# Casts and scaling on GpSimd, twelve output products beside steps 10 to 15, and loads ordered behind transfers in a windowed attention

## The chip, the cores and the metric

The kernel runs on one core of one Trainium2 chip. A core has a matrix engine (TensorE, PE in the profile, with PEld for its weight loads), a vector engine (VectorE, DVE), an activation engine (ScalarE, ACT), a general engine (GpSimd, POOL) and an engine that here only starts transfers (SyncE, SP). Each engine works through its own list of instructions in order, and waits on semaphores for what other engines and transfers give it. They share an on-chip memory of 128 partitions (SBUF); TensorE writes its products to eight banks of accumulators (PSUM), which VectorE and ScalarE read. The metric is the device time of one launch in microseconds (us), and lower is better; each figure is a median of several runs.

## The reference

A trunk of two layers for one sequence of 512 tokens and 1024 features. Layer 0 mixes tokens by a gated unit; layer 1 by attention. Both then have a gated feed-forward part with a short convolution and a gated embedding. What matters here is layer 1's attention, cut to its core:

```python
q = (xn @ w_q).reshape(B, nb, BLOCK, N_KV_HEADS, GQA_GROUP, HEAD_DIM)
scores = einsum('bnikgd,bnjkd->bnkgij', q, kblk) * HEAD_DIM ** -0.5
scores = scores - slopes * dist           # a slope per head, distance in tokens
scores = where(valid, scores, -inf)       # window of 128, causal
m = maximum(max(scores), sink)            # a learned sink per head
e = exp(scores - m)
probs = e / (sum(e) + exp(sink - m))
out = einsum('bnkgij,bnjkd->bnikgd', probs, vblk)
return out.reshape(B, S, 1024) @ w_o
```

There are 16 query heads of 64 features in four groups; each group shares one head of keys and values. Tokens stand in four blocks of 128; a block sees itself and the block before it.

## The kernel before, in words

**Products of three.** Every float32 matrix is split into a high part (rounded to the type that TensorE multiplies fast, F32R) and a low part, the rest. A product of two is then three matmuls: high by high, high by low, low by high (`mm3`, line 175). Activations carry the letters h and l (`oh`, `ol` are the high and low half of attention's output, `o2` their list by 128 features: two to a head group). Weights come from HBM as float32.

**The planner of weights.** `pieces` lists all weight pieces in the order of use, 1 MB each as a rule; a piece has two units of 128x1024. `load` (line 122) starts a piece's transfer on SyncE's queue into a raw buffer (`wraw`). `pump` (line 133) makes the next units ready: `wh`, a cast on ScalarE (line 154), and `wl`, a subtraction on VectorE (line 155); it calls `load` for the piece that it needs. Four `wh` and four `wl` buffers go round. `chunk` hands a piece's units to the products. In attention's steps there is one raw buffer (`state["tags"] = [0]`), so that a load waits until both units of the piece before it have been subtracted.

**Attention's steps.** There are 16 steps, i = 4 g + n, for head group g and token block n. The loop from line 864 traces in each turn i: `scores(i)`; `fill(i)`, other products to lie beside the step; `mix(i - 2)`; `turn(i - 1)`; `weights(i)`. The loop ends two turns later, so 16 and 17 have no scores.

- `scores` (767): eight score products on TensorE (`sc`), a masked copy and four fused reductions with the slope on VectorE (784, 788; they write `prs`), four exponentials with their sums on ScalarE (793).
- `weights` (797): reciprocals of the sums, and the scaling of the four heads' 128x128 probabilities, the first on VectorE (807), three on ScalarE (805).
- `turn` (816): four transposes on TensorE (`tr`, 822), their split into `ph` and `pl` (ScalarE 252, VectorE 253), and for all but a sequence's first block two selections on GpSimd (830) for the block before.
- `mix` (835): two or four products with the values (`pv`, 844), a copy on ScalarE (848), two additions on VectorE (852), the high half `oh` on ScalarE (856) and the low half `ol` on GpSimd (857; the last step's on VectorE).

**What lies beside the steps.** The table `beside` (733) gives `fill` its work. Steps 0 to 9: `project`, the query products of groups 1 to 3 (`q`), 24 beside steps 0 and 1, and 12 beside each of 2 to 9. With a half group's last product `queries` (641) scales the result, splits it on ScalarE (657) and VectorE (658), and starts four transfers on SyncE's queue (661, 662), which lay the high and low halves out over the partitions; a group's scores need those of both halves. From step 10 on: `merge(m, k0, k1)` (720), the output products of 128 features m (`o`) over the inputs k0 to k1, three matmuls for each k. Inputs 2 g and 2 g + 1 are head group g's, so they need all four blocks' mixes of that group. A started `o` keeps its PSUM bank until its last product, behind the loop (line 884). `more` pumps one unit.

**Who sets the order.** A scheduler orders each engine's instructions at build time by priority, which is about the order of the program's text, and by when it expects operands and buffers to be free. `tc.high_priority()` moves scores, turn and weights ahead. So a step's scores can pass products that were traced before them, loads can pass transfers, and a product that is expected late is put behind others. On the chip the order is fixed.

Of the kernel before, what the change touches and what calls it, by code (L numbers as in the profile page):

```python
# [48 lines left out]
def tile_yoco(ctx: ExitStack, tc: tile.TileContext, t, out: bass.AP, out_b: bass.AP):  # L49
# [67 lines left out]

    units = [(i, q, lo, n) for i, p in enumerate(pieces) for q, (lo, n) in enumerate(p[2])]
    raws, ready = {}, {}
    state = {"raw": 0, "unit": 0, "next": 0, "tags": [0, 1, 2], "turn": 0, "pt": 0}  # L120

    def load(upto, queue=nc.sync):
        while state["raw"] < min(upto, len(pieces)):
            j = state["raw"]
            a, m = pieces[j][:2]
            tags = state["tags"]
            r = wp.tile([P, 2 * UNIT], F32, tag=f"r{tags[state['turn'] % len(tags)]}", bufs=1, name=f"wraw{j}")
            state["turn"] += 1
            queue.dma_start(r[:, :m].rearrange("p (c m) -> p c m", c=2) if j in paired else r[:, :m], a)
            raws[j] = r  # L130
            state["raw"] += 1

    def pump(upto):
        while state["unit"] < min(upto, len(units)):
            i, q, lo, n = units[state["unit"]]
            load(i + 1)
            u = state["unit"]
            own = pieces[i][3]
            if own:
                pool, *tags = own[q]  # L140
                wh, wl = (pool.tile([P, n], F32R, tag=tg, name=f"own{u}_{tg}") for tg in tags)
            else:
                wh = wp.tile([P, UNIT], F32R, tag="wh", bufs=WBUFS, name=f"wh{u}")
                wl = wp.tile([P, UNIT], F32R, tag="wl", bufs=WBUFS, name=f"wl{u}")
            if i in paired:
                whole = raws[i][:, : pieces[i][1]].rearrange("p (c k n) -> p k c n", c=2, n=256)
                src = whole[:, lo // S : (lo + n) // S]
                hi, low = (x[:, :n].rearrange("p (k c n) -> p k c n", c=2, n=256) for x in (wh, wl))
            else:
                src, hi, low = raws[i][:, lo : lo + n], wh[:, :n], wl[:, :n]  # L150
            if u == 0:
                nc.vector.tensor_copy(hi, src)
            else:
                nc.scalar.copy(hi, src)  # L154
            nc.vector.tensor_sub(low, src, hi.bitcast(F32))  # L155
            ready[u] = (wh, wl, n)
            state["unit"] += 1
# [17 lines left out]
    def mm3(ps, parts, xs, c0, n=P, first=True, last=True):  # L175

        for k, ((wh, wl, off), (xh, xl)) in enumerate(zip(parts, xs)):
            a, b = off + c0, off + c0 + n
            st = first and k == 0
            en = last and k == len(parts) - 1  # L180
            nc.tensor.matmul(ps, wh[:, a:b], xh, start=st, stop=False)  # L181
            nc.tensor.matmul(ps, wh[:, a:b], xl, start=False, stop=False)  # L182
            nc.tensor.matmul(ps, wl[:, a:b], xh, start=False, stop=en)  # L183

    def mm3t(ps, xs, parts, c0, n, tok, first=True, last=True):

# [454 lines left out]
    def queries(ps, g, j):  # L641
# [17 lines left out]
        for e, q in enumerate(res):  # L659
            me, it = sides[e], sides[1 - e]  # L660
            nc.sync.dma_start(q[me, :].bitcast(F32), hi[me, :])
            nc.sync.dma_start(q[it, :].bitcast(F32), qf[me, :])
        return res

    qs = {0: []}
# [63 lines left out]
    def more():  # L729
# [12 lines left out]
        7: [(project, 3, 0, 4, 8), (more,)],  # L742
        8: [(project, 3, 1, 0, 4)],
        9: [(project, 3, 1, 4, 8)],
        10: [(merge, 0, 0, 3), (more,)],
        11: [(merge, 0, 3, 4), (merge, 1, 0, 2), (more,)],
        12: [(merge, 1, 2, 4), (merge, 2, 0, 1)],
        13: [(merge, 2, 1, 4)],
        14: [(merge, 0, 4, 6), (merge, 1, 4, 6)],
        15: [(merge, 2, 4, 6)],  # L750
        16: [(merge, 3, 0, 6)],
        17: [(merge, 4, 0, 6)],
    }

    def fill(i):
        for f, *args in beside.get(i, []):
            f(*args)

    o2 = [[ap.tile([P, S], F32R, tag=f"a{x}{m}", name=f"o{x}{m}") for x in "hl"] for m in range(KD)]
    steps = [(g, n) for g in range(GROUPS) for n in range(NC)]  # L760
    live = {}
# [5 lines left out]
    def scores(i):  # L767
# [8 lines left out]
        for b in range(2):  # L776
            sc = psum(f"sc{i}_{b}").rearrange("p (e h k) -> p e h k", e=2, h=2)
            for j in range(2):
                o = sc[:, j].rearrange("p h k -> p (h k)")[:, :nk]
                q = qs[g][2 * b + j][:, n * P : (n + 1) * P]  # L780
                nc.tensor.matmul(o, q, kh[g // 2][:, g % 2, t0 : t0 + nk], start=True, stop=False)
                nc.tensor.matmul(o, q, kl[g // 2][:, g % 2, t0 : t0 + nk], start=False, stop=True)
# [14 lines left out]
    def weights(i):  # L797
# [4 lines left out]
        for e in range(GQ):  # L802
            a, r = pr[:, e, :P], ds[:, e : e + 1]
            if e:
                nc.scalar.activation(a, a, AF.Copy, scale=r)
            else:
                nc.vector.tensor_scalar_mul(a, a, r)
        live[i] = pr

    def pair(name):  # L810
# [45 lines left out]
            nc.scalar.copy(oh[:, cols], o[:, b, :])  # L856
            (nc.vector if i == last - 1 else nc.gpsimd).tensor_sub(ol[:, cols], o[:, b, :], oh[:, cols].bitcast(F32))

    last = len(steps)
    side = at.tile([P, 4 * S], F32, tag="vtl", name="side")  # L860
    fill(-1)
    state["tags"] = [0]
    pts4 = wp.tile([P, 4, S], F32R, tag="r1", bufs=1, name="pts4")
    for i in range(last + 2):
        if i < last:
            with tc.high_priority():
                scores(i)
# [242 lines left out]
```

## Time and profile before

| What | Value |
|---|---|
| median of 3 runs | 1141.03 us (1140.64 to 1141.64) |
| the profiled execution's own time | 1141.22 us |
| its span in the profile | 1139.5 us |
| granted TensorE clock | 0.998 |
| attention's steps, first scores to the last mix | about 591.8 to 686.3 us |

The profile is of one execution. Its page gives each engine's busy time; views of the trace give groups of instructions, stretches of time and single instructions with what ended the idle time before them ("0.80 <-DVE prs L807": 0.80 us idle, ended by VectorE's instruction of line 807 that writes `prs`). A matmul's duration overlaps that of the next, so the cost of one is the distance from start to start. Names come without buffer numbers: `wraw`, `wh`, `o`. L12 is line 12 of the kernel.

### The profile page before, as it was taken

How to read it: one execution, taken by the hardware profiler on the slowest of the kernel's cores; microseconds unless marked ns; L12 is line 12 of the kernel's file. 1: busy time of each engine (PE TensorE's matmuls, PEld its weight loads, DVE VectorE, ACT ScalarE, POOL GpSimd, SP SyncE). 2: the span in 40 equal slices, each digit the busy share in tenths (PEclk: the TensorE clock that was granted, in tenths of full speed). 3: DMA queues.
4: the chain of work that ended last, by engine and by line, in shares of the span. 5: the costliest groups of instructions: out<-in, count | busy, mean ns of one | idle time of the engine just before them, and what ended most of it. 6: DMA issues, size and time to landing. Idle time of an engine off the chain costs nothing.

```text
span 1139.5 us, 13604 instructions
## 1 busy us (share of the span) xinstructions
PE 1127.0 (99%) x5266; PEld 940.5 (83%) x5266; DVE 749.6 (66%) x1158; ACT 530.0 (47%) x875; POOL 107.7 (9%) x175
## 2 busy tenths in 40 slices
PE   9999999999999999999999999999999999999997
PEld 7888888888888888888898878888888888888896
DVE  7366477763677367557988977777636763675675
ACT  6533344441344234445657985444313432355562
POOL 2000200000000000021213343000000000000222
PEclk9999999999999999999999999999999999999999
DMA  8422323223223322432224315223223233224302
GB/s 298 145 83 74 111 75 111 101 85 111 78 98 102 111 76 86 134 107 79 74 75 129 93 38 185 98 88 111 78 107 110 66 102 111 93 80 160 111 1 75
DMA packets 25776, 115.41 MB, mean 101 GB/s; under 512 B 2920, under 2 KB 8176, under 8 KB 16240
## 3 DMA queue, kind: packets, MB, share of 16 engines
q1 hardware_dynamic: 25152, 113.89, 29.8%
q8 instruction: 41, 0.67, 0.2%
q10 hardware_dynamic: 560, 0.66, 0.2%
q14 instruction: 23, 0.19, 0.1%
HBM read 108.24 MB, written 2.11 MB: 97 GB/s over the span
## 4 chain that ended last, share of the span: by engine, by line
PE 95%; DVE 2%; issue 1%; ACT 1%; DMA 1%; POOL 0%; SPq 0%; POOLq 0%; DVEq 0%; ACTq 0%
PE up L181 14%; PE up L183 14%; PE up L182 14%; PE d L183 8%; PE d L181 8%; PE d L182 8%; PE gate L181 2%; PE gate L183 2%; PE gate L182 2%; PE u L182 1%; PE u L183 1%; PE u L181 1%; PE o L182 1%; PE o L181 1%; PE o L183 1%; PE q L181 1%
## 5 line engine op out<-in xcount | busy, mean ns | idle before, releaser
L154 ACT CAST wh<-wraw 128x1024 fp32r<-128x1024 f32 (+2 forms) x197 | 202.0, 1028 | 264.6 <-PE d L182 131.0
L155 DVE TENSOR_TENSOR wl<-wraw,wh 128x1024 fp32r<-128x1024 f32 (+1 forms) x198 | 238.4, 1205 | 127.9 <-ACT wh L154 127.6
L181 PE MATMUL up<-nf00h,wh 128*128 128x512 f32 x352 | 137.1, 390 | 0.0
L181 PE MATMUL up<-nf10h,wh 128*128 128x512 f32 x352 | 137.0, 389 | 0.0
L182 PE MATMUL up<-nf00l,wh 128*128 128x512 f32 x352 | 136.9, 389 | 0.0
L183 PE MATMUL up<-nf00h,wl 128*128 128x512 f32 x352 | 136.9, 389 | 0.0
L183 PE MATMUL up<-nf10h,wl 128*128 128x512 f32 x352 | 136.9, 389 | 0.0
L182 PE MATMUL up<-nf10l,wh 128*128 128x512 f32 x352 | 136.9, 389 | 0.0
L181 PE MATMUL d<-ah,wh 128*128 128x512 f32 x352 | 136.9, 389 | 0.0
L182 PE MATMUL d<-al,wh 128*128 128x512 f32 x352 | 136.9, 389 | 0.0
L183 PE MATMUL d<-ah,wl 128*128 128x512 f32 x352 | 136.9, 389 | 0.0
L379 ACT ACTIVATE c<-hs,vec 128x512 f32<-128x512 f32 x88 | 71.5, 815 | 72.0 <-DVE hs L375 71.2
L380 DVE SCALAR_TENSOR_TENSOR c<-hs,vec,c 128x511 f32<-128x511 f32 x88 | 65.8, 749 | 34.5 <-ACT c L379 34.4
L355 DVE TENSOR_TENSOR h<-h,d 128x512 f32<-128x512 f32 x56 | 38.4, 686 | 73.8 <-PE d L183 73.8
L252 ACT CAST ah<-a 128x512 fp32r<-128x512 f32 x44 | 27.4, 622 | 109.5 <-DVE a L385 109.4
L183 PEld LDWEIGHTS up<-nf10h,wl 128*128 128x128 f32 x352 | 66.1, 188 | 13.8
L182 PEld LDWEIGHTS d<-al,wh 128*128 128x128 f32 x352 | 66.1, 188 | 13.8
L183 PEld LDWEIGHTS up<-nf00h,wl 128*128 128x128 f32 x352 | 66.1, 188 | 13.8
L183 PEld LDWEIGHTS d<-ah,wl 128*128 128x128 f32 x352 | 66.1, 188 | 13.7
L182 PEld LDWEIGHTS up<-nf00l,wh 128*128 128x128 f32 x352 | 66.1, 188 | 13.7
L182 PEld LDWEIGHTS up<-nf10l,wh 128*128 128x128 f32 x352 | 66.1, 188 | 13.7
L181 PEld LDWEIGHTS d<-ah,wh 128*128 128x128 f32 x352 | 66.1, 188 | 13.6
(454 smaller groups left out, 2061.7 us busy)
## 6 DMA issues: line engine op xcount, KB each, us to landing
wraw<-in_w_up SPq DMA_DIRECT2D x44, 1024.0 KB, 4.8
wraw<-in_w_down SPq DMA_DIRECT2D x16, 896.0 KB, 4.6
wraw<-in_w_down SPq DMA_DIRECT2D x8, 1024.0 KB, 4.8
wraw<-in_w_gate SPq DMA_DIRECT2D x8, 1024.0 KB, 4.8
wraw<-in_w_u SPq DMA_DIRECT2D x4, 1024.0 KB, 5.9
wraw<-in_w_out SPq DMA_DIRECT2D x4, 1024.0 KB, 4.8
wraw<-in_w_q SPq DMA_DIRECT2D x4, 1024.0 KB, 4.9
wraw<-in_w_o SPq DMA_DIRECT2D x4, 1024.0 KB, 4.9
```

Source lines behind the costliest of these rows:

```text
L154: nc.scalar.copy(hi, src)
L155: nc.vector.tensor_sub(low, src, hi.bitcast(F32))
L181: nc.tensor.matmul(ps, wh[:, a:b], xh, start=st, stop=False)
L182: nc.tensor.matmul(ps, wh[:, a:b], xl, start=False, stop=False)
L183: nc.tensor.matmul(ps, wl[:, a:b], xh, start=False, stop=en)
L252: nc.scalar.copy(hi, src)
L355: nc.vector.tensor_add(h[m], h[m], ps)
L379: nc.scalar.activation(c, hs, AF.Identity, bias=v("conv_b", l * 2 * NJ + col), scale=cw[2])
L380: nc.vector.scalar_tensor_tensor(c[:, 1:], hs[:, : S - 1], cw[1], c[:, 1:], op0=ALU.mult, op1=ALU.add)
```

## The change

Four things are changed, all in attention's steps.

1. The cast of a weight unit (line 154) is taken from `state["cast"]`: GpSimd's copy in the turns 1 to 14, ScalarE's in all others and outside the loop. Nine units are pumped in those turns.
2. The scaling of a step's first head moves from VectorE's `tensor_scalar_mul` to GpSimd's `tensor_mul`, in all 16 steps.
3. The table gives steps 10 to 15 twelve products each and pumps a unit more in step 12; steps 16 and 17 take `o4` and `o5` where they took `o3` and `o4`. Two orders on TensorE are added, without a semaphore: a step's first product of `mm3` comes behind the last score product that was traced before it (`front`, in every step), and a step's first score product comes behind the last product of the step before (`filled`, behind the steps 10 to 15).
4. The first load traced after a half group's queries comes behind the last of its four transfers in SyncE's queue (`sent`).

```diff
-    state = {"raw": 0, "unit": 0, "next": 0, "tags": [0, 1, 2], "turn": 0, "pt": 0}
+    state = {"raw": 0, "unit": 0, "next": 0, "tags": [0, 1, 2], "turn": 0, "pt": 0, "sent": None, "front": None, "rear": None, "filled": None, "cast": nc.scalar.copy}
+
+    def behind(ins, front):
+
+        tc.add_manual_dep(ins.ins, front.ins.name,
+                          mybir.DependencyInfo(mybir.DependencyClass.NoSync, mybir.DependencyReason.DATA),
+                          reason="order")
...
-            queue.dma_start(r[:, :m].rearrange("p (c m) -> p c m", c=2) if j in paired else r[:, :m], a)
+            ins = queue.dma_start(r[:, :m].rearrange("p (c m) -> p c m", c=2) if j in paired else r[:, :m], a)
+            if state["sent"] is not None:
+                behind(ins, state["sent"])
+                state["sent"] = None
...
-                nc.scalar.copy(hi, src)
+                state["cast"](hi, src)
...
-            nc.tensor.matmul(ps, wh[:, a:b], xh, start=st, stop=False)
+            ins = nc.tensor.matmul(ps, wh[:, a:b], xh, start=st, stop=False)
+            if state["front"] is not None:
+                behind(ins, state["front"])
+                state["front"] = None
             nc.tensor.matmul(ps, wh[:, a:b], xl, start=False, stop=False)
-            nc.tensor.matmul(ps, wl[:, a:b], xh, start=False, stop=en)
+            state["rear"] = nc.tensor.matmul(ps, wl[:, a:b], xh, start=False, stop=en)
...
-            nc.sync.dma_start(q[it, :].bitcast(F32), qf[me, :])
+            state["sent"] = nc.sync.dma_start(q[it, :].bitcast(F32), qf[me, :])
...
-        10: [(merge, 0, 0, 3), (more,)],
-        11: [(merge, 0, 3, 4), (merge, 1, 0, 2), (more,)],
-        12: [(merge, 1, 2, 4), (merge, 2, 0, 1)],
-        13: [(merge, 2, 1, 4)],
+        10: [(merge, 0, 0, 2), (merge, 1, 0, 2), (more,)],
+        11: [(merge, 0, 2, 4), (merge, 1, 2, 4), (more,)],
+        12: [(merge, 2, 0, 4), (more,)],
+        13: [(merge, 3, 0, 4)],
         14: [(merge, 0, 4, 6), (merge, 1, 4, 6)],
-        15: [(merge, 2, 4, 6)],
-        16: [(merge, 3, 0, 6)],
-        17: [(merge, 4, 0, 6)],
+        15: [(merge, 2, 4, 6), (merge, 3, 4, 6)],
+        16: [(merge, 4, 0, 6)],
+        17: [(merge, 5, 0, 6)],
...
+        if 9 < i < last:
+            state["filled"] = state["rear"]
+
+    last = GROUPS * NC
...
-                nc.tensor.matmul(o, q, kh[g // 2][:, g % 2, t0 : t0 + nk], start=True, stop=False)
-                nc.tensor.matmul(o, q, kl[g // 2][:, g % 2, t0 : t0 + nk], start=False, stop=True)
+                ins = nc.tensor.matmul(o, q, kh[g // 2][:, g % 2, t0 : t0 + nk], start=True, stop=False)
+                if state["filled"] is not None:
+                    behind(ins, state["filled"])
+                    state["filled"] = None
+                state["front"] = nc.tensor.matmul(o, q, kl[g // 2][:, g % 2, t0 : t0 + nk], start=False, stop=True)
...
-                nc.vector.tensor_scalar_mul(a, a, r)
+                nc.gpsimd.tensor_mul(a, a, r.to_broadcast([P, P]))
...
+        state["cast"] = nc.gpsimd.tensor_copy if 0 < i < last - 1 else nc.scalar.copy
...
+    state["cast"] = nc.scalar.copy
```

More of the change, by code (lines that the diff above doesn't have):

```diff
@@ L857, in mix @@
             (nc.vector if i == last - 1 else nc.gpsimd).tensor_sub(ol[:, cols], o[:, b, :], oh[:, cols].bitcast(F32))
-    last = len(steps)
     side = at.tile([P, 4 * S], F32, tag="vtl", name="side")
```

## The prediction

> **What bounds the kernel now.** First the page: its engine line, and the chain of work that ended last.
>
> ```profile
> span 1139.5 us, 13604 instructions
> ...
> PE 1127.0 (99%) x5266; PEld 940.5 (83%) x5266; DVE 749.6 (66%) x1158; ACT 530.0 (47%) x875; POOL 107.7 (9%) x175
> ...
> PE 95%; DVE 2%; issue 1%; ACT 1%; DMA 1%; POOL 0%; SPq 0%; POOLq 0%; DVEq 0%; ACTq 0%
> ```
>
> TensorE sets the end and has 12.5 us without work (1139.5 - 1127.0). The change adds and removes no product, so it can win only places where PE waits, and lose by making new ones. The second view, busy time by stretch, shows where such places lie in attention.
>
> ```profile
> core 0: us, PE busy (x) PEld busy (x) DVE busy (x) ACT busy (x) POOL busy (x), PEclk, DMA share, GB/s
> ...
> 635.00:645.00 10.00, 10.00 (x58) 8.57 (x57) 8.77 (x30) 9.90 (x35) 4.51 (x10) 1.00 0.47 150
> 645.00:655.00 10.00, 8.72 (x50) 6.93 (x49) 9.67 (x38) 9.30 (x31) 4.52 (x10) 1.00 0.24 52
> 655.00:665.00 10.00, 8.82 (x47) 6.75 (x48) 9.59 (x38) 9.84 (x41) 4.91 (x10) 1.00 0.30 102
> 665.00:675.00 10.00, 8.81 (x50) 6.81 (x49) 7.73 (x31) 8.65 (x30) 4.06 (x9) 1.00 0.02 6
> 675.00:685.00 10.00, 9.98 (x46) 7.91 (x45) 5.58 (x10) 5.87 (x16) 4.56 (x7) 1.00 0.07 10
> ```
>
> Up to 645 PE is full although ScalarE is at 9.9 of 10. From 645 to 675 VectorE and ScalarE stay near full and PE drops to 8.8: there the steps have little besides their own work. The clock is 1.00 throughout. The third view, PE's instructions in order of time, gives each hole its size.
>
> ```profile
> 648.11 0.39 PE L181 MATMUL o<-oh,wh 128*128 128x512 f32 x1
> ...
> 649.50 0.39 PE L844 MATMUL pv<-pts,vt 128*128 128x512 f32 x1
> 650.68 0.41 PE L822 MATMUL tr<-ident,prs 128*128 128x128 f32 x2 [0.80 <-DVE prs L807]
> ...
> 653.74 0.71 PE L844 MATMUL pv<-pts,vt 128*128 128x512 f32 x2
> 654.93 0.53 PE L822 MATMUL tr<-ident,prs 128*128 128x128 f32 x3 [0.48 <-DVE prs L807]
> ...
> 657.60 0.43 PE L844 MATMUL pv<-pts,vt 128*128 128x512 f32 x1
> 658.50 0.55 PE L822 MATMUL tr<-ident,prs 128*128 128x128 f32 x3 [0.47 <-DVE prs L807]
> ...
> 660.90 0.49 PE L181 MATMUL o<-oh,wh 128*128 128x512 f32 x1
> 662.11 0.50 PE L182 MATMUL o<-ol,wh 128*128 128x512 f32 x1 [0.71 <-POOL ol L857]
> ...
> 664.05 0.39 PE L181 MATMUL o<-oh,wh 128*128 128x512 f32 x1
> 664.28 0.39 PE L182 MATMUL o<-ol,wh 128*128 128x512 f32 x1
> ...
> 669.10 0.40 PE L844 MATMUL pv<-pts,vt 128*128 128x512 f32 x1
> 670.03 0.52 PE L822 MATMUL tr<-ident,prs 128*128 128x128 f32 x3 [0.53 <-DVE pts L253]
> ...
> 671.56 0.28 PE L782 MATMUL sc<-kl,q 128*128 128x256 f32 x1
> 672.20 0.47 PE L844 MATMUL pv<-p13h,vt 128*128 128x512 f32 x1 [0.36 <-ACT prs L793]
> 672.92 0.50 PE L181 MATMUL o<-oh,wh 128*128 128x512 f32 x1 [0.26 <-ACT oh L856]
> ```
>
> Start to start, a 512-column product costs 0.23 us (664.05 to 664.28). What a row takes beyond that is lost: 0.95 (649.50 to 650.68), 0.73 (two products from 653.74 to 654.93), 0.67, 0.98, then 0.70, 0.52 (a 256-column product, taken at 0.12) and 0.49. The first four make **3.3 us** in steps 10 to 13, the last three **1.7 us** in steps 14 and 15: 5.0 us together, and the most that this change can win but for crumbs.
>
> **The change, part by part.**
>
> *Twelve products a step.* Twelve take 12 x 0.23 = 2.8 us, where steps 10 to 13 have nine in their list. The score products come one step ahead of the transposes that need their weights, so three products more a step (0.7 us) give the waits above (0.5 to 0.8 idle) what they lack. I let all 5.0 us go, and now ask what is late next; both new order rules matter for it. A step's products come behind its scores, and from 10 to 15 the next scores come behind those products, so a product that isn't ready holds up everything.
>
> *Step 11* takes k = 2 and 3: the outputs of heads' group 1, finished by step 7's mix. Step 14 takes k = 4 and 5, finished by step 11's mix, whose products end just ahead of it (the row at 669.10 is at their end). How long a mix needs until its low half is there:
>
> ```profile
> 661.60 1.71 POOL L857 TENSOR_TENSOR ol<-side,oh 128x128 fp32r<-128x128 f32 x4
> ...
> 672.95 0.46 POOL L857 TENSOR_TENSOR ol<-side,oh 128x128 fp32r<-128x128 f32 x1 [0.51 <-ACT oh L856]
> ```
>
> At 669.10 + 0.23 step 11's mix has left PE, and the first low half is there at 672.95 + 0.46: 4.1 us. The scores of step 15 cannot be put in between any more. What may: step 12's mix (two products, 0.46) and step 13's transposes (0.5), so a hole of 4.1 - 1.0 = 3.1 us. With VectorE and ScalarE relieved and no scores of 15 in their queues it may be 1.5. I take **2.6**, near the row. The four pieces from 661.60 are those of steps 7 and 8, a long way behind their mixes, since VectorE and ScalarE take the marked (high priority) work first. A pinned order limits how far that can run away; the price of it stands with the loads, since both waits fall in the same place.
>
> *Loads behind the transfers.* This moves SP's queue. Four loads follow a half group of queries in the program's text; today they leave ahead of its four transfers, now they stay behind them:
>
> ```profile
> 589.18 12.83 SPq L129 DMA_DIRECT2D wraw<-in_w_q  x2
> 603.51 0.47 SPq L661 DMA_DIRECT2D q<-qhi  x1
> ...
> 605.40 0.70 SPq L662 DMA_DIRECT2D q<-qf  x1
> ```
>
> ```profile
> 633.39 0.33 SPq L129 DMA_DIRECT2D wraw<-in_w_o  x1
> ...
> 651.77 1.10 SPq L662 DMA_DIRECT2D q<-qf  x2
> ```
>
> ```profile
> DMA to landing us min/median/max: 4.7/5.0/5.5
> ```
>
> ```profile
> 608.73 0.39 PE L181 MATMUL q<-n11h,wh 128*128 128x512 f32 x1
> ...
> 611.45 0.39 PE L844 MATMUL pv<-pts,vt 128*128 128x512 f32 x1
> ```
>
> Today the query weights of heads' group 2 leave at 589.18 and those of group 3 at 601.7 (the row's last), ahead of the transfers at 603.51. Now the first of these leaves behind the transfer that ends at 606.1, lands at 606.1 + 5.0 = 611.1, and has still to be cast and subtracted. PE wants it at 608.73. With the cast at 1.3 (below) the first two products can go at 612.4, the third, which reads the low half, at 613.6. Between 608.73 and 611.45 PE today does those twelve products (2.7 us); other work that is ready instead: step 0's mix (0.46), step 1's transposes (0.5), step 3's scores (eight at 0.12): 1.9 us. The hole: 612.4 - 608.7 - 1.9 = 1.8, and 0.7 for the low half: **2.5**, which I take. Bounds: 1.1 (step 2's transposes and step 1's mix, 1.4 us more, come forward as well) and 4.4 (nothing does).
>
> The load of group 3's weights moves from 601.7 behind the transfers of group 2's first half. Those twelve products more end about a step behind 611.45, at 616, and transfers leave some 4 us behind their products (group 1's second half, 24 products or 5.5 us, ends at 608.73; a step's scores and transposes, 1.4, lie ahead of it, so its first half ended at 601.8, and those transfers were out at 606.1): 620, landed 625, cast and subtracted 628. Its products are four steps of 5.1 us (12 x 0.23 and 2.3 of the step's own) behind 608.73, at 629, and any hole before moves both: 0. The third load, the first piece of the output weights, has until step 10, at 648.1: 0. The fourth, the second piece of the output weights (o2 and o3), moves from 633.39 to behind 651.77 + 1.10 = 652.9, lands at 657.9, and is cast and subtracted at 660.4. Step 12 wants it: from 648.1, where step 10's products begin, two times twelve products (5.5) and two steps' own work (1.9 each: scores 0.95, transposes 0.5, rest of a mix) make 657.4, its low half 0.5 later. So steps 11 and 12 together wait 2.5 us, for step 7's mix or for the weights; relieved queues could send the transfers 1.5 us earlier, which leaves 1.0. I take **1.8**, the middle.
>
> *GpSimd's casts and scaling.* Rows of the stretch from 595 to 690, grouped:
>
> ```profile
> L857 POOL TENSOR_TENSOR ol<-side,oh 128x128 fp32r<-128x128 f32 x30 | 14.1, 490 | 4.3 <-ACT oh L856 4.2
> ...
> L155 DVE TENSOR_TENSOR wl<-wraw,wh 128x1024 fp32r<-128x1024 f32 x10 | 12.2, 1221 | 4.5 <-ACT wh L154 4.5
> ...
> L154 ACT CAST wh<-wraw 128x1024 fp32r<-128x1024 f32 x10 | 10.4, 1042 | 0.7 <-PE o L182 0.5 <-DMA wraw<-in_w_q 0.2
> ...
> L807 DVE TENSOR_SCALAR prs<-prs,ds 128x128 f32<-128x128 f32 x16 | 6.5, 409 | 0.2
> ...
> L830 POOL TENSOR_SCALAR_AFFINE_SELECT pts<-pts 128x512 fp32r<-128x512 f32 x8 | 5.5, 681 | 7.0 <-ACT pts L252 6.4 <-DVE pts L253 0.5
> ```
>
> ScalarE loses nine casts of the ten (9 x 1.04 = 9.4 us), VectorE sixteen scalings (6.5 us). GpSimd has no cast of this size; the nearest with one input is the selection, 0.68 for 512 columns, twice that is 1.3; the two-input row (0.49 for 128) would make it 3.9. I take 1.3. The scaling is the two-input kind and shape of L857: 0.49, beside ScalarE's three scalings of the same step, so hidden unless something stands ahead of it in GpSimd's queue. A cast that waits for its load stands there with all behind it: scaling, selections and low halves, and PE's transposes and products wait for those. I take **0.5** for it; bounds -1 (the relieved queues) and 5 (rival below).
>
> [...]
>
> **The sum:** -5.0 + 2.6 + 2.5 + 1.8 + 0.5 = +2.4. On the profiled execution (1141.22: the span and 1.7 around it) 1143.6; on the median, 0.2 below it, **1143.4 us**. Bounds: 3.1 + 4.4 + 2.5 + 0.5 - 5.0 = +5.5 with the upper ends of the three holes, 1.5 + 1.1 + 1.0 - 1.0 - 5.0 = -2.4 with the lower.
>
> **The rivals.**
>
> *The holes are filled (faster).* The order on PE is made with the loads' times known, so steps 1 and 2 come forward and hide the first load (1.1, or 0.6 where a scores' step more is found); relieved queues bring step 7's and step 11's halves sooner (1.0 and 1.3) and the scaling off VectorE ends the waits named L807. It decides at 612.4: if transposes and scores of two steps lie ahead of it, the hole is about 1. Sum: -5.0 + 0.8 + 1.0 + 1.2 - 0.8 = -2.8: 1138.2. For it: all of 595 to 645 runs without a hole on twelve products a step. Against it: those steps' products never depended on a mix.
>
> *An exchange (no change).* The first load is hidden, and the pinned order gives back at 11, 12 and 14 what twelve products win: -5.0 + 1.1 + 1.8 + 2.2 = 0.1: 1141.1.
>
> *GpSimd becomes the bound (slower still).* Its work for a step is 0.88 + 1.3 + 0.2 + 0.49 = 2.9 us; one cast at 3.9, or one that stands waiting for a load, makes 6.8, over the 5.1 us that PE needs (2.8 for twelve products, 2.3 own): 1.7 a time. Three such steps beyond the sum (5.1): 1148.5. Against it: GpSimd is at 4 to 5 of 10.
>
> **How the numbers follow.** Forecast 0.40, GpSimd 0.12, exchange 0.18, filled holes 0.30. I call anything within 0.2% (2.3 us: 1138.7 to 1143.3) the same, about what a measurement of this kernel can tell. The forecast's own spread, its bounds narrowed to 1142.0 to 1146.0, puts a quarter of it within that; the exchange leaves a ninth on each side, the filled holes a fifteenth within. Faster 0.28 + 0.02 = 0.30, same 0.10 + 0.14 + 0.02 = 0.26, slower 0.30 + 0.02 + 0.12 = 0.44. The range, 1137.0 to 1147.0, takes in the filled holes but for 0.06 and leaves out 0.10 of GpSimd's case and 0.02 of the forecast's.
>
> **What would show it.** In the profile after: PE waits for a cast or a subtraction at about 609 to 613 (right), or transposes and scores of steps 1 to 3 lie there without a hole (wrong by up to 2.5). A wait for ol or oh ahead of the first k = 4 product of 2 to 3 us; one of wl or ol in steps 11 and 12. L807 as a releaser of tr gone. GpSimd's cast at 1.3, and its scaling's wait below 0.5. If PE is full from 645 to 675, the forecast is wrong and the time is near 1138.

## The result and the profile after

| | median, us | ratio to before, 95% interval |
|---|---|---|
| before | 1140.98 (1140.64 to 1141.64) | |
| forecast | 1143.4 (1137.0 to 1147.0) | |
| after | 1158.17 (1156.99 to 1158.75) | 1.0149 (1.0131 to 1.0166) |

The sign was forecast, the size was not: 17.2 us are lost where 2.4 were expected, far outside the range. The profiled execution took 1156.99 us. Its page, the engine line and the chain of work that ended last:

```profile
span 1155.1 us, 13599 instructions
...
PE 1133.7 (98%) x5266; PEld 944.0 (82%) x5266; DVE 747.1 (65%) x1142; ACT 523.9 (45%) x867; POOL 125.8 (11%) x199
...
PE 90%; DVE 4%; ACT 2%; DMA 2%; issue 1%; POOL 1%; SPq 0%; POOLq 0%; DVEq 0%; ACTq 0%
```

TensorE is without work for 21.4 us (before 12.5), and with the same products it is busy for 6.7 us more: it waits more, and it is slower for a while. The waits, PE's instructions in order of time (start, duration, line; in brackets the idle time and what ended it; `mm3` now has the lines 190, 194, 195):

```profile
608.35 0.39 PE L195 MATMUL q<-n11h,wl 128*128 128x512 f32 x1
612.06 0.57 PE L190 MATMUL q<-n11h,wh 128*128 128x512 f32 x1 [3.32 <-ACT wh L163]
...
613.32 0.80 PE L195 MATMUL q<-n11h,wl 128*128 128x512 f32 x1 [0.26 <-DVE wl L164]
...
643.79 0.30 PE L796 MATMUL sc<-kh,q 128*128 128x128 f32 x1 [1.48 <-DMA q<-qf]
...
662.84 0.50 PE L862 MATMUL pv<-pts,vt 128*128 128x512 f32 x1 [2.32 <-ACT pts L264]
...
681.29 0.73 PE L862 MATMUL pv<-pts,vt 128*128 128x512 f32 x2 [1.08 <-DVE pts L265]
684.10 0.80 PE L190 MATMUL o<-oh,wh 128*128 128x512 f32 x1 [1.56 <-ACT oh L874]
685.29 0.79 PE L194 MATMUL o<-ol,wh 128*128 128x512 f32 x1 [0.39 <-POOL ol L875]
...
733.62 0.40 PE L314 MATMUL nf1ms<-nf1quarter,alike 128*128 128x16 f32 x2 [1.34 <-DVE nf1quarter L306]
```

The row at 612.06 is the forecast's first hole; nothing came forward to fill it. The wait at 643.79 (step 8's scores, for the queries' transfers), the one at 662.84 and the last stand in no term of the sum. The holes named L807 are gone, as forecast.

How far the kernel has fallen behind, at the starts of products that both have, counted from the first score product of each: 5.5 us at step 1's transposes, 7.2 at step 7's, 13.5 at the feed-forward part's first product, 15.7 from its first product with `w_down` (`d`) to the end.

The slowness shows in the windows view, cut at the places where the granted clock changes (stretch, its length, busy time and count of PE, PEld, DVE, ACT, POOL, then the granted clock, DMA share, GB/s):

```profile
608.94:612.35 3.41, 0.29 (x1) 0.30 (x2) 1.59 (x3) 1.66 (x2) 1.04 (x1) 1.00 0.61 205
612.35:615.77 3.42, 3.16 (x8) 1.99 (x8) 2.04 (x2) 0.00 (x0) 0.00 (x0) 0.50 0.46 102
615.77:619.18 3.41, 3.41 (x23) 2.96 (x22) 1.00 (x3) 0.88 (x2) 0.58 (x1) 1.00 0.00 0
...
660.13:663.55 3.42, 1.10 (x9) 0.70 (x7) 2.58 (x8) 3.13 (x12) 1.25 (x4) 1.00 0.90 188
663.55:666.96 3.41, 3.41 (x11) 2.66 (x9) 2.64 (x12) 2.90 (x12) 2.30 (x6) 0.50 0.64 262
...
680.61:684.03 3.42, 1.25 (x6) 0.72 (x6) 3.38 (x13) 2.63 (x12) 0.58 (x2) 1.00 0.01 2
684.03:687.44 3.41, 2.94 (x6) 2.05 (x7) 1.76 (x5) 2.19 (x8) 3.40 (x7) 0.50 0.48 151
687.44:690.86 3.42, 3.42 (x11) 2.74 (x11) 0.00 (x0) 0.00 (x0) 0.00 (x0) 0.50 0.37 156
690.86:694.27 3.41, 3.41 (x19) 2.92 (x19) 2.07 (x11) 1.66 (x8) 0.00 (x0) 1.00 0.02 5
```

Behind each of the three large holes TensorE gets half its clock for 3.41 or 6.83 us. Start to start, a 512-column product takes 0.43 us there (688.02 to 688.45) and 0.23 at full clock (692.35 to 692.58), so half of TensorE's busy time there, (3.16 + 3.41 + 2.94 + 3.42) / 2 = 6.5 us, is the estimated price. SyncE's queue shows the loads behind the transfers; the rows of before are in the prediction (the first two loads left from 589.18 on; the third, which has no row there, at 613.33):

```profile
604.58 1.19 SPq L674 DMA_DIRECT2D q<-qf  x2
605.83 0.58 SPq L135 DMA_DIRECT2D wraw<-in_w_q  x1
...
625.66 0.55 SPq L135 DMA_DIRECT2D wraw<-in_w_q  x1
...
640.69 2.08 SPq L135 DMA_DIRECT2D wraw<-in_w_o  x1
...
661.61 23.18 SPq L135 DMA_DIRECT2D wraw<-in_w_o  x3
```

GpSimd's new work, grouped, from 595 to 690:

```profile
L163 POOL CAST wh<-wraw 128x1024 fp32r<-128x1024 f32 x8 | 8.2, 1038 | 4.9 <-DMA wraw<-in_w_q 3.7 <-DMA wraw<-in_w_o 1.2
L825 POOL TENSOR_TENSOR prs<-prs,ds 128x128 f32<-128x128 f32 x15 | 6.0, 399 | 0.3 <-DVE ds L819 0.2
```

A cast takes 1.04 us, as on ScalarE (1.3 was taken), the scaling 0.40 (0.49 was taken). The casts are eight: the turns 1 to 14 pump eight units, and seven with the old table, not the nine that the texts ahead and some expectations below name.

### The profile page after: what moved, and what is told of

Its sections match the earlier page's. It is cut to its first block, busy times and chain, and to the rows that moved or that the text cites. A ratio compares the mean times of both kernels' runs of the same rounds, so it can differ in the third digit from the quotient of the medians.

```text
span 1155.1 us, 13599 instructions
## 1 busy us (share of the span) xinstructions
PE 1133.7 (98%) x5266; PEld 944.0 (82%) x5266; DVE 747.1 (65%) x1142; ACT 523.9 (45%) x867; POOL 125.8 (11%) x199
## 4 chain that ended last, share of the span: by engine, by line
PE 90%; DVE 4%; ACT 2%; DMA 2%; issue 1%; POOL 1%; SPq 0%; POOLq 0%; DVEq 0%; ACTq 0%
PE up L195 14%; PE up L194 14%; PE up L190 14%; PE d L194 8%; PE d L195 8%; PE d L190 8%; PE gate L190 2%; PE gate L194 2%; PE gate L195 2%; PE u L194 1%; PE u L190 1%; PE u L195 1%; DVE wl L164 1%; PE q L195 1%; PE q L190 1%
## 5 line engine op out<-in xcount | busy, mean ns | idle before, releaser
L163 ACT CAST wh<-wraw 128x1024 fp32r<-128x1024 f32 (+2 forms) x189 | 193.7, 1027 | 263.1 <-PE d L194 131.3
L190 PEld LDWEIGHTS up<-nf00h,wh 128*128 128x128 f32 x352 | 66.1, 188 | 13.7
L190 PEld LDWEIGHTS up<-nf10h,wh 128*128 128x128 f32 x352 | 66.1, 188 | 13.7
```

Of the source, the lines that this page charges most:

```text
L163: state["cast"](hi, src)
L190: ins = nc.tensor.matmul(ps, wh[:, a:b], xh, start=st, stop=False)
```

## The experiments

Each time is the median of at least four executions, and the kernel before was run beside each set (1141.06 to 1141.28). Edits are against the kernel after the change unless "before" is said. Line numbers differ by a few from kernel to kernel. Waits and windows are those of one profiled execution of each kernel. Single executions of a kernel lie up to 4.7 us apart (1143.07 to 1147.81 with loads free and no pinned order), so a difference of 2 us between two rows of the table is to be read with their intervals.

| Kernel | us | ratio to before (95%) |
|---|---|---|
| before + ordered loads | 1152.36 | 1.0096 (1.0079 to 1.0113) |
| before + GpSimd's casts and scaling | 1144.24 | 1.0033 (1.0023 to 1.0043) |
| before + table and pinned order | 1150.61 | 1.0082 (1.0067 to 1.0097) |
| after, loads free | 1146.53 | 1.0051 (1.0036 to 1.0066) |
| after, no pinned order | 1155.86 | 1.0130 (1.0113 to 1.0147) |
| after, loads free, no pinned order | 1144.23 | 1.0033 (1.0023 to 1.0044) |
| after, only the first load ordered | 1156.00 | 1.0128 (1.0113 to 1.0143) |
| after, only the other three ordered | 1151.55 | 1.0090 (1.0072 to 1.0108) |
| after, first hole filled with products | 1155.37 | 1.0123 (1.0108 to 1.0139) |
| before + casts | 1144.92 | 1.0029 (1.0017 to 1.0041) |
| before + scaling | 1141.36 | 1.0001 (0.9991 to 1.0010) |
| before + table | 1145.90 | 1.0040 (1.0025 to 1.0055) |
| before + table + scaling | 1144.14 | 1.0023 (1.0014 to 1.0033) |
| the same + norm's order | 1141.38 | 1.0001 (0.9991 to 1.0010) |
| the same + 3 casts | 1141.06 | 1.0003 (0.9994 to 1.0011) |
| the same + 5 casts | 1141.53 | 1.0006 (0.9997 to 1.0015) |
| after + ScalarE's order | 1157.34 | 1.0144 (1.0128 to 1.0161) |

### The parts by themselves

**Ordered loads on the kernel before:** `sent` with its edge, and nothing else of the change.

> The kernel of before with one part of the change: the first load after each half group's transfers stays behind them in SyncE's queue. Casts on ScalarE, scaling on VectorE, the old table, no pinned order on TensorE. Theory (late loads make the first two holes): the hole ahead of group 2's query products comes, with a stretch of halved clock behind it, about 5.4 us as in the changed kernel, and about 1.6 at step 8's scores: 1147 to 1150 us against 1141. Rival (the holes come from GpSimd standing in a cast that waits, not from the load): ScalarE or VectorE pick the unit up in time and the loads cost at most 1 us: 1142 or less. Second rival: the waiting cast now stands in ScalarE's queue ahead of exponentials, so it costs more than in the changed kernel: 1151 or more.

1152.36: +11.3, dearer than the theory. The first hole is there (3.26 us idle) without GpSimd. The wait at step 8's scores is not there; step 12's scores wait 1.74 us for their transfers instead (at 664.24). The time is within the second rival's bound, but its ground isn't there: the row at 612.06 above shows that the first unit's cast is ScalarE's in the changed kernel too, and the ordered loads cost as much there (below).

**GpSimd's part on the kernel before:** `state["cast"]` and `nc.gpsimd.tensor_mul`, nothing else.

> The kernel of before with one part of the change: nine casts and the sixteen first-head scalings on GpSimd, nothing else. Theory (GpSimd's work is cheap and hidden, cast 1.04, scaling 0.40): within 1.5 us of before, 1139.5 to 1142.5, no halved clock. Rival (GpSimd becomes the bound): holes in front of transposes and mixes named after GpSimd, 1146 or more.

+3.1: between the theory's bound and the rival's. The profiled execution has no half clock within attention.

**Table and pinned order on the kernel before:**

> The kernel of before with one part of the change: the table of twelve products beside steps 10 to 15 with its two pinned orders on TensorE; loads free, casts on ScalarE, scaling on VectorE. Theory (the pinned first products of k = 4 wait for step 11's mix; the hole and the halved clock behind it cost 6 us, the start of the feed-forward part 2, and up to 5.0 of the old holes go): 1143 to 1147. Rival (the table only fills the old holes, and the late piece of the output weights makes what is seen at the k = 4 products): 1136 to 1139.

+9.5, worse than both the theory and the rival allow.

**Loads free in the changed kernel:**

```diff
-            if state["sent"] is not None:
-                behind(ins, state["sent"])
-                state["sent"] = None
```

> The changed kernel with the loads free to pass the transfers again, all else as in the change. Theory: the first hole with its halved clock (5.4) and the wait at step 8's scores (1.6) go, and part of the holes in steps 11 and 12: 1147 to 1151 against 1158. Rival (holes move on and come back at the next wait): 1155 or more.

1146.53, 11.6 under the changed kernel: the first hole and more. In both companies the ordered loads cost 11.3 to 11.6 us, two thirds of the loss. The wait at step 8's scores stays (1.92 us), so it needs no ordered load.

### The pinned order

```diff
-            if state["front"] is not None:
-                behind(ins, state["front"])
-                state["front"] = None
...
-                if state["filled"] is not None:
-                    behind(ins, state["filled"])
-                    state["filled"] = None
```

> The changed kernel without the two pinned orders on TensorE; the table, the ordered loads and GpSimd's work stay. The scheduler puts step 15's scores and step 13's mix ahead of the first k = 4 products again. Theory (the pinned order keeps ready work behind products that wait for step 11's mix): the hole at these products with its halved clock, 6.2 us in the changed kernel, falls to 2 or 3: 1153 to 1155.5. Rival (VectorE and ScalarE are what is late, so whatever stands there waits as long): 1157 or more.

> The changed kernel with loads free and without the two pinned orders: twelve products a step and GpSimd's casts and scaling only. Theory: 3 us under the kernel that has only the loads free (1146.5), so 1142.5 to 1144.5. Rival (what is left is GpSimd's part, which cost 3.1 by itself, and the table's own lateness): 1146 or more.

1155.86 and 1144.23: the pins, as the two orders are called from here on, cost 2.3 us with the loads ordered and 2.3 with them free; in both pairs the intervals overlap. With free loads the theory's place is right: the waits of 0.50, 1.93 and 0.31 us at these products shrink to one of 0.40. With ordered loads the gain is just below what the theory asked for, and the wait hardly shrinks: without the pins step 12's mix waits 2.56 us there for VectorE's split, where the rows from 681.29 to 685.29 add up to 3.03. The half clock behind it lasts 3.41 instead of 6.83 us, and that is most of the gain. So for the wait the rival holds in this company.

### The loads one by one

**The first alone** (group 2's query weights), then **the other three alone** (`if g == 1` in the same place):

```diff
             state["sent"] = nc.sync.dma_start(q[it, :].bitcast(F32), qf[me, :])
+        if g > 1:
+            state["sent"] = None
```

> The changed kernel with one load alone behind its transfers, that of group 2's query weights; the other three are free. Theory (each late load costs by itself): 5.4 over the kernel with all loads free, 1151 to 1153. Rival one (the first hole makes all that follows late): 1157 or more. Rival two (what the first hole loses is slack that later waits give back): 1148 to 1150.

> The changed kernel with the first of the four loads free and the other three behind their transfers: the counterpart of the run that had the first alone. Theory (the first load is nearly the whole price of the ordered loads, 9.5 of 11.6; the others have slack once group 2's weights are early): 1146 to 1149, no hole ahead of group 2's products. Rival (prices do not add up, each late load by itself is enough to put steps 9 to 13 behind): 1153 or more, the wait at step 8's scores and the one in step 9 to 11 as in the changed kernel.

1156.00 and 1151.55: 9.5 and 5.0 us over free loads. The first expectation (5.4 for the hole) was too low, and so was the second. They are not additive (14.5 against 11.6). With the first load alone, PE is 6.4 us behind at step 1's transposes, and loses more in step 11, where products need step 7's mix:

```profile
661.27 0.50 PE L190 MATMUL o<-oh,wh 128*128 128x512 f32 x1 [0.67 <-ACT oh L876]
662.93 0.80 PE L194 MATMUL o<-ol,wh 128*128 128x512 f32 x1 [1.16 <-POOL ol L877]
```

With the other three alone no product waits long for a weight, and step 8's scores don't wait; the long waits are those for the split probabilities in steps 9 and 12 (2.32 and 2.14 us) and one of 1.56 for step 11's mix. What turned in the changed kernel is ScalarE's list:

```profile
661.19 0.98 ACT L823 ACTIVATE prs<-prs,ds 128x128 f32<-128x128 f32 x3 [0.24 <-DVE ds L819]
662.20 0.58 ACT L264 CAST pts<-tr 128x512 fp32r<-128x512 f32 x1
```

With loads free:

```profile
657.22 0.59 ACT L261 CAST pts<-tr 128x512 fp32r<-128x512 f32 x1
657.70 0.99 ACT L820 ACTIVATE prs<-prs,ds 128x128 f32<-128x128 f32 x3
```

The scheduler, which places every engine's instructions by expected times, put step 10's exponentials and scalings ahead of step 9's split when the loads were ordered. **That order set back** for steps 9 and 10 (`ins` is a scaling, `split` the cast of the turn before):

```diff
+                if i in (9, 10):
+                    behind(ins, state["split"])
```

> The changed kernel with one more order, on ScalarE: the scalings of steps 9 and 10 stand behind the split of the step before, as in the kernel of before and in the changed kernel with free loads. Theory (with the loads pinned, the scheduler turned this order round on ScalarE, and that, not a load, is what step 9's mix waits 2.3 us for, with half a clock behind it): that wait and the stretch of half clock at 664 go, 1154 to 1156 against 1158.2. Rival (ScalarE is as late with either order, so the next product that needs step 7's mix waits instead): 1157 or more.

1157.34, 0.8 us less and within the spread of the changed kernel's executions (1156.99 to 1158.75): by the time the rival. The wait for the split is gone with the half clock behind it, and 1.56 us for step 7's mix stand in its place:

```profile
661.59 0.50 PE L190 MATMUL o<-oh,wh 128*128 128x512 f32 x1 [1.56 <-ACT oh L877]
```

At the feed-forward part's first product this execution is 1.6 us ahead of the changed kernel's (724.69 against 726.04, counted from the first score product of each). Then it loses this again in a half-clocked stretch behind the norm that the changed kernel doesn't have:

```profile
733.40:736.81 3.41, 3.41 (x10) 2.66 (x9) 1.54 (x4) 0.00 (x0) 1.02 (x1) 0.50 0.06 24
```

So the order is worth about 1.6 us where it stands, and the time doesn't show it. It is a small part of what the loads cost: ScalarE and VectorE are late there with both orders. Why the three later loads make them so was not separated further.

### The clock

**Fifteen products of 512 columns**, whose result is written over, in the first hole; mix 0, transposes 1 and scores 3 are held behind group 2's products, so that the order of all others stays:

```diff
             box["qp"] = psum(f"q{g}_{j}")
+            if (g, j) == (2, 0):
+                for _ in range(15):
+                    nc.tensor.matmul(box["qp"], xq[0][0][:, :P], xq[0][0], start=True, stop=True)
```

> The changed kernel with fifteen products of 512 columns, whose result is written over, in TensorE's queue ahead of group 2's first query product, where the first hole lies; the order of all others is kept. Theory (a hole of 3.5 us is what halves the granted clock behind it): the clock stays at 1.00 from 612 to 616, and with half of 3.41 us won the time is 1156 to 1157 against 1158.2. Rival (the clock falls for another reason): the same stretch of half clock, 1158 or more.

1155.37, 2.8 us less. The same two stretches in its windows view:

```profile
608.90:612.31 3.41, 3.41 (x16) 2.56 (x15) 1.66 (x3) 1.67 (x2) 1.04 (x1) 1.00 0.56 192
612.31:615.72 3.41, 2.88 (x13) 2.13 (x12) 1.94 (x2) 0.00 (x0) 0.00 (x0) 1.00 0.48 106
```

Group 2's first product starts at 611.91, with the weights no sooner there than before, yet the clock stays at 1.00. The stretch ahead has 3.41 us busy where the changed kernel has 0.29, so here the empty stretch made the half clock. More was won than the 1.6 of half clock in the first stretch; steps behind it moved too.

### Casts, scaling and table apart

> The kernel of before with the nine casts on GpSimd and nothing else. Theory (a cast that waits in GpSimd's queue for its load or its buffer puts VectorE's subtraction later, and that in front of the queries' scaling and split, so the transfers that step 8's scores need leave late): the wait at these scores, 1.06 and 0.39 with casts and scaling together, is there, 1142 to 1144. Rival (the scaling is what costs): 1140.5 to 1141.5, no wait there.

> The kernel of before with the first head's scaling on GpSimd and nothing else. Theory (0.40 us beside ScalarE's three scalings, VectorE relieved of 6.5 us): 1139 to 1141. Rival (it stands behind selections and low halves in GpSimd's queue, so transposes come late, as the 1.85 in step 10 with casts and scaling together): 1142.5 to 1144.

1144.92 and 1141.36: the casts cost 3.7 us, more than the theory's 1144 allows, the scaling nothing that can be measured. Of the casts' waits, two on PE and what SyncE's queue shows:

```profile
637.75 0.30 PE L790 MATMUL sc<-kh,q 128*128 128x128 f32 x1 [0.77 <-DVE side L861]
...
658.50 0.45 PE L790 MATMUL sc<-kh,q 128*128 128x128 f32 x1 [1.47 <-DMA q<-qf]
```

```profile
650.89 1.10 SPq L667 DMA_DIRECT2D q<-qhi  x2
656.20 1.10 SPq L668 DMA_DIRECT2D q<-qf  x2
```

In the kernel before, the low halves of group 3 leave at 651.77 (a row of the prediction), 1.5 us behind the high ones:

```profile
650.24 1.10 SPq L661 DMA_DIRECT2D q<-qhi  x2
```

With the casts on GpSimd it is 5.3 us, and step 12's scores wait for them (658.50). VectorE subtracts the low half at 655.49, before at 651.06; a weight's subtraction (649.06) now lies ahead of it. The casts don't fill GpSimd (busy for 5.72 and 6.54 of 10 us from 635 to 655); they change when VectorE gets to its other work. Behind the wait the clock is halved for 6.83 us (658.20 to 665.02), by half the busy time an estimated 3.3 of the 4.6 us that this execution (1145.76) loses.

> The kernel of before with the table of twelve products and nothing else: no pinned order, loads free, casts on ScalarE, scaling on VectorE. Theory (without the pins the scheduler keeps unready products out of the way; of the 5.0 us in old holes most go, the feed-forward part's start gives 2.2 back): 1138.5 to 1141. Rival (the table itself wants mixes and weights that VectorE and ScalarE cannot finish earlier): 1145 or more, near the 1150.6 with pins.

> The kernel of before with the table of twelve products and the first head's scaling on GpSimd; casts on ScalarE, loads free, no pinned order. Theory: the lowest of the parts put together, no wait at step 8's scores, 1138 to 1140.5. Rival (ScalarE, with its casts, is what steps 10 to 13 wait for): 1143 or more, and the casts on GpSimd would be worth having.

1145.90 and 1144.14. The table by itself loses 4.7 us where the sum had it win 5.0; both times lie in the range of their rival. What the rivals gave as the reason, the steps' own engines, covers a part only: 2.8 us of the second's loss go with one order at the start of the feed-forward part (below). The pins beside it without GpSimd cost 4.7 more (1150.61). The scaling, worth nothing by itself, wins 1.8 beside the table (the two intervals overlap). With GpSimd's casts too it is 1144.23: the casts neither cost nor win there.

### The start of the feed-forward part

In the kernel with table and scaling PE waits at the end of attention too, and pays half a clock for it. PE's row, then VectorE's, then the windows view:

```profile
720.65 0.40 PE L308 MATMUL nf1ms<-nf1quarter,alike 128*128 128x16 f32 x2 [1.34 <-DVE nf1quarter L300]
```

```profile
714.58 1.55 DVE L161 TENSOR_TENSOR wl<-wraw,wh 128x1024 fp32r<-128x1024 f32 x1 [0.71 <-ACT wh L160]
...
716.65 1.21 DVE L161 TENSOR_TENSOR wl<-wraw,wh 128x1024 fp32r<-128x1024 f32 x1
...
719.91 0.69 DVE L300 TENSOR_REDUCE nf1quarter<-nf1turn 128x16 f32<-128x512 f32 x1
```

```profile
652.98:656.39 3.41, 1.94 (x12) 1.38 (x11) 2.98 (x11) 3.34 (x12) 1.82 (x4) 1.00 0.93 262
656.39:659.80 3.41, 3.41 (x10) 2.66 (x11) 3.04 (x15) 3.17 (x16) 2.25 (x5) 0.50 0.29 118
...
717.83:721.24 3.41, 1.71 (x8) 0.85 (x7) 2.85 (x6) 0.18 (x1) 0.00 (x0) 1.00 0.69 226
721.24:724.65 3.41, 3.41 (x10) 2.65 (x9) 2.03 (x7) 0.00 (x0) 1.02 (x1) 0.50 0.20 82
```

The table takes eighteen products (`o5`, k = 0 to 5, 4.1 us) from behind attention. There they had covered VectorE's subtractions of the next weights: in the kernel before the norm's product (718.13) waits for nothing. **Those two subtractions behind the norm's reduction** (`low`, which is traced ahead of the feed-forward part for it):

```diff
             nc.vector.tensor_sub(low, src, hi.bitcast(F32))
+            if u in (127, 128):
+                behind(ins, state["low"])
```

> The kernel with table and scaling alone (1144.1) and one more order: behind attention the last two weight subtractions of VectorE's list stand behind the norm's last steps instead of between them. Theory (with fewer products left behind attention, VectorE's subtractions 1.2 us each make the norm late, and TensorE waits for it at the feed-forward part's start, 2.0 us): that wait goes, 1141.5 to 1142.5. Rival (VectorE's or GpSimd's whole list there is late, so the wait only moves): 1143.7 or more.

1141.38, 2.8 us less. The wait for the reduction falls from 1.34 to 0.36 us:

```profile
718.41 0.40 PE L310 MATMUL nf1ms<-nf1quarter,alike 128*128 128x16 f32 x2 [0.36 <-DVE nf1quarter L302]
```

The rest of the 2.8 is the clock: the four executions of the kernel with table and scaling that have a mean clock of 0.998 or more take 1142.46 to 1142.99 us, and the profiled one (1145.51, 0.996) has two halved stretches, only one of them behind the norm.

Table and scaling then neither win nor lose. A wait and two stretches of this kernel:

```profile
654.39 0.49 PE L855 MATMUL pv<-pts,vt 128*128 128x512 f32 x1 [1.04 <-ACT pts L260]
```

```profile
645.00:655.00 10.00, 8.85 (x50) 7.17 (x48) 9.68 (x32) 9.36 (x33) 5.00 (x11) 1.00 0.31 69
655.00:665.00 10.00, 9.30 (x48) 7.59 (x49) 6.53 (x27) 9.20 (x33) 5.29 (x13) 1.00 0.24 97
```

With twelve products a step PE still waits, now for the splits. Its idle time from 645 to 675 is 2.4 us against 3.7 before. ScalarE is busy for 9.36 and 9.20 of 10 us, VectorE for 9.68 and then only 6.53.

**A better kernel?** On top of it, casts on GpSimd from turn 8 on (three of them), and from turn 5 on (five):

```diff
-        state["cast"] = nc.gpsimd.tensor_copy if 0 < i < last - 1 else nc.scalar.copy
+        state["cast"] = nc.gpsimd.tensor_copy if 8 <= i < last - 1 else nc.scalar.copy
```

> The kernel with table, scaling on GpSimd and the norm's order (1141.4), and now three of the nine casts on GpSimd, those of the output weights' later units, pumped in steps 10 to 12; the six before them stay on ScalarE. Theory (ScalarE and VectorE are full in steps 7 to 11 and set their pace; a cast there on GpSimd relieves ScalarE, and with the early ones left on ScalarE nothing makes the queries' transfers late): 1139 to 1140.8, less than before. Rival (a cast on GpSimd puts VectorE's subtraction and GpSimd's own low halves back as much as ScalarE wins): 1141.2 to 1142.5.

> The same with five casts on GpSimd: also the two of the output weights' first piece, pumped in steps 6 and 7. Theory: a further relief of ScalarE in steps 7 to 9, 1138.5 to 1140.8. Rival (these two stand where they hold up step 8's scores, as all nine did): 1142 or more with a wait at these scores.

1141.06 and 1141.53, neither to be told from before. With five, PE again loses time between step 8's score products (1.74 and 0.41 us beyond their own from start to start), with three it doesn't: the output weights' first two casts are the ones that hold these scores up. With three, ScalarE is busy for 8.30 and 7.45 of 10 us in the two stretches above, and the time is the same. So a full ScalarE is not shown to be what PE waits for; that a step's chain from scores to split simply takes this long fits too, and no run separates the two. No kernel of this study is faster than before.

## Why the prediction was wrong

The parts in a row, each on top of the one before, against the terms of the sum:

| Part | forecast | measured | from |
|---|---|---|---|
| old holes filled (table, scaling; norm in order) | -5.0 | +0.1 | 1141.38 - 1141.28 |
| start of the feed-forward part | 0 | +2.8 | 1144.14 - 1141.38 |
| GpSimd's casts | in +0.5 | +0.1 | 1144.23 - 1144.14 |
| products for step 11's mix (pins) | +2.6 | +2.3 | 1146.53 - 1144.23 |
| ordered loads | +2.5 + 1.8 | +11.6 | 1158.17 - 1146.53 |
| sum | +2.4 | +16.9 | |

The rows depend on their order. Each alone on the kernel before, ordered loads, GpSimd's part and the table with its pins cost 11.3, 3.1 and 9.5 us, 23.9 together, where all in one cost 17.2.

**"I let all 5.0 us go"** failed. The step before it read the holes as a lack of products ("three products more a step give the waits above what they lack"). The windows of before already had VectorE at 9.67 and 9.59 of 10 and ScalarE at 9.30 and 9.84 in those stretches, and the prediction quoted them. ("Near full" holds up to 665; from there to 675 they were at 7.73 and 8.65.) The runs show that more products were not enough: the old releaser L807 goes, the splits take its place, and PE's idle time in these stretches falls by 1.2 us, 3.7 to 2.4. The sum's 5.0, counted from start to start, was more than that idle time. Whether the load of the two engines or the length of the chain through them sets the step stays open.

**"What may come forward"** failed for the first load. The landing and the cast were right (612.06 for 612.4); of the 1.9 us of other work that was to hide the hole, none stood there. The forecast had this as its upper bound, 4.4; measured at step 1's transposes it is 5.5, with the half clock, which no term had. The text took the middle of its bounds because work was ready; but the scheduler had put that work behind these products in both kernels, and on the chip the order is fixed.

**The later loads at 0, 0 and 1.8** failed: 5.0 together. The text had looked at the loads' slack and not at that of the transfers behind them: with ordered loads on the kernel before, step 12's scores wait 1.74 us for theirs. The changed kernel's wait at step 8's scores looks the same but is not shown to be the loads': it is there with loads free (1.92) and with the casts alone (0.77), and not with ordered loads alone. In step 11 of the changed kernel neither a weight nor step 7's mix was waited for first, but ScalarE's split; with ScalarE's order set back it was step 7's mix, as forecast.

**"A hole of 4.1 - 1.0 = 3.1, I take 2.6"**: the wait was right, 1.56 and 0.39 idle at 684.10 and 685.29, 1.08 at 681.29. But the 1.08 is that of step 12's mix, which was to fill the hole; it waits for its own split, with or without the pins. The pins cost 2.3 in this company, 4.7 beside the table alone.

**GpSimd at +0.5**: right in this company, by luck: by themselves casts and scaling cost 3.1, the casts alone 3.7. The casts were eight where the sum counted nine. The gain that the lower bound allowed shows beside the table (1.8, with overlapping intervals). The rival "GpSimd becomes the bound" lay nearest in time (1148.5) but not in mechanism: GpSimd is not full (busy for 52.6 of 99 us from 591 to 690), and no PE wait of the changed kernel is ended by a GpSimd cast. Its 6.8 us also counted the cast twice: 0.88 + 3.9 + 0.2 + 0.49 is 5.5, 0.4 above PE's 5.1. The scaling, with two inputs, took 0.40 where 0.49 was forecast; VectorE's own instruction, with one input and a scalar, took 0.41.

**Left out altogether**: the start of the feed-forward part, since the products moved there were priced as gain only; and the clock, an estimated 6.5 us of the changed kernel, which is spread over the rows of the table above.

## What to carry to other kernels

Before filling a hole on the engine that sets the end, look at the engines that feed it in the same stretch: if they are nearly full, more work there may fill little (1.2 of 3.7 us here), and the work is missed where it was taken from. A transfer that is made to wait is priced by the fixed order behind its first user, not by what would be ready, and by the transfers and casts that come after it in turn. A hole of some 1.5 us on TensorE should be priced with what a halved clock may take behind it: behind the 1.34 us ahead of 720.65, in the kernel with table and scaling, the clock was at 0.50 for 3.41 us.

## What the runs showed of the hardware

**In these traces the granted clock changed by stretches of 3.41 us, and it was halved behind partly idle ones.** In the changed kernel the half-clocked stretches begin at 612.35, 663.55 and 684.03: 15 and 6 times 3.41 apart. Cut on that grid, the stretch ahead of a halved one has PE busy for 0.29, 1.10 and 1.25 us, and 1.94 and 1.71 in the kernel with table and scaling. Stretches with 2.66, 2.69 and 2.07 (changed kernel) are followed by full clock. No sharp limit shows: stretches with 1.62 (from 652.66, only the other three loads ordered) and 1.94 (from 651.92, with the norm's order) kept the full clock, 2.01 (from 652.94, with 3 casts) didn't. The rows of the changed kernel:

```profile
639.65:643.07 3.42, 2.66 (x17) 2.16 (x15) 3.31 (x13) 3.35 (x14) 2.13 (x5) 1.00 0.62 138
643.07:646.48 3.41, 2.69 (x13) 2.32 (x14) 2.67 (x11) 3.38 (x13) 2.26 (x5) 1.00 0.90 298
...
731.82:735.23 3.41, 2.07 (x10) 1.42 (x10) 2.31 (x7) 0.00 (x0) 0.42 (x1) 1.00 0.90 308
735.23:738.64 3.41, 3.41 (x17) 2.80 (x16) 2.40 (x5) 1.05 (x1) 0.60 (x1) 1.00 0.00 0
```

At half clock a stretch with 3.16 busy was enough to get the full clock back in the changed kernel, one with 2.94 was not; with loads free even 3.35 was not (from 638.55). So in the changed kernel's trace a hole's price hung on where it lay on the grid: the wait of 1.48 us ahead of 643.79 falls across a border (643.07), with 2.66 and 2.69 us busy on its two sides, and halves nothing. The table-and-scaling kernel's executions go from 1142.46 us at a mean clock of 0.998 to 1145.51 at 0.996.

**In the changed kernel a GpSimd cast from float32 to F32R was as fast as ScalarE's**: 1.04 us for 128x1024 on both from 595 to 690 (the mean of eight and of two). One cast of the kernel with the casts alone took 2.08 (608.76); why is not shown.
